# A hybrid decoder trunk: triangular blocks inverted by columns, projection results taken one block later, and a further weight slot

## The chip, the cores and the metric

The kernel runs on one core of one Trainium2 chip. The metric is the device time of one execution, in microseconds (us).

## The reference, cut to what matters

Two post-norm layers over 512 tokens of width 1024. Layer 0 mixes tokens with an RWKV-7 recurrence (8 heads of 64) beside a gated spatial unit; layer 1 with latent attention. Each layer then attends to 256 memory tokens and applies a mixture of 32 experts, of which each token takes two.

```python
def rwkv7_recurrence(r, w, k, v, kk, a):
    def step(state, inp):
        r_t, w_t, k_t, v_t, kk_t, a_t = inp
        sa = jnp.einsum('bhvk,bhk->bhv', state, -kk_t)
        state = (state * w_t[:, :, None, :]
                 + sa[..., None] * (kk_t * a_t)[:, :, None, :]
                 + v_t[..., None] * k_t[:, :, None, :])
        return state, jnp.einsum('bhvk,bhk->bhv', state, r_t)
...
    h = layer_norm(DN_ALPHA * h + mix, ln1_g[layer], ln1_b[layer])
    xa = mem_cross_attention(h, mem, ...)
    h = layer_norm(DN_ALPHA * h + xa, ln2_g[layer], ln2_b[layer])
    ff = hier_moe(h, ...)       # top-1 of 4 groups, top-2 of 8 SwiGLU experts
    h = layer_norm(DN_ALPHA * h + ff, ln3_g[layer], ln3_b[layer])
```

The kernel computes the recurrence in chunks of 128 tokens. For each of 32 pairs (4 chunks, 8 heads) it needs the inverse of a 128 x 128 unit triangular matrix, I minus the strictly triangular part of a product of decayed keys.

## The kernel before

**The mixer's first part** (`mixer`, up to L1019) has two generators that are traced in turns. `prep` (L831 to L943) makes the inverses. It normalises keys (tiles kk, KR, Bn), multiplies them into pab (L872), copies these to Aab, collects the 32 x 32 diagonal blocks in b8 and transposes them (L878, L879), and puts a copy in PSUM (pd). Then it solves all 128 diagonal blocks at once on VectorE, by rows: row i of the inverse (in t8, called tr) is the sum over earlier rows times the entries of row i, one or two products and one reduction for each i (L886 to L893). Four transposes place the blocks in TT, one puts the other orientation in b8 (L900, L902). Larger blocks follow on TensorE: 32 to 64 (pC, pT, L905 to L925), 64 to 128 (pC2, pN2, pT2, L928 to L943), each with copies out of PSUM, most of them on ScalarE. Trace names: pC stands for pC and pC2, pT for pT and pT2, pN for pN2.

`filler` (L1001) is the work that TensorE has meanwhile: projections of x through the columns of `ab_w_in`, in blocks of 128 columns (`proj_cm`, 24 matmuls of 128x512 each, as every fp32 product is made of three). In order: one block for the gate (take_g), four for r (take_r), four for v, then `spatial`: a position-major projection (`proj_tm`, tile ptm, 96 matmuls) whose gelu z is normalised on VectorE, and four blocks with `gate`, which multiply z into pz. Each block's weights are cast on ScalarE (L218) and their low part is made by GpSimd (L219) before the matmuls. `consume` takes the result of a block at once: for r this is a scaling on ScalarE (L760), a shift on VectorE (L761), the product bt (L951) and eight small matmuls into pbn (L956).

**Order.** The framework's planner sets one fixed order for each engine, from the order in which instructions are traced and from when its own durations have their inputs ready. An engine then works its queue strictly in that order. PSUM has two tags of four banks: "a" for `prep`, "b" for `filler`.

**The expert stages** (`moe`) stream 192 weight tiles of 1 MB through a ring of slots, issued by SyncE's queue in the order of use. `wtile` takes the slot at the head of the ring and, unless it is used once only, puts it back at the end. 18 slots are used again and again; two more (the later places of wy and wc) serve one load each. So `ExpertWeights` has n = 20, issues n - 1 loads ahead, and the twentieth when its place is free. Ahead of each stage, `Router` keeps transposed token tiles hT in two half-slots, tags last0 and last1, of which the second first holds the router's weights. At the end of layer 0's stage `early_keys` computes layer 1's memory keys and uses the same two half-slots for kTe.

Of the kernel before, what the change touches and what calls it, by code (L numbers as in the profile page):

```python
# [421 lines left out]

def early_keys(k, l, tag):

    p = k.router.p
    mh, ml = (k.wtile(n, F32R).rearrange("p (k n) -> p k n", k=KD) for n in ("mh", "ml"))
    k.lo_eng, k.nsplit = k.nc.gpsimd, 0
    load_split(k, k.A["memT"], mh, ml, KD, 256)
    yield
    for b, _ in enumerate(memory_keys(k, l, None, lambda h: p.tile([P, D], F32R, name=f"kTe{h}", tag=f"last{h % 2}", bufs=1), mh, ml, tag)):  # L430
        if b == 3:
            k.lo_eng = k.nc.vector
    k.lo_eng, k.nsplit = k.nc.vector, 4
# [126 lines left out]
class Router:  # L560
# [4 lines left out]
    def __init__(self, k, rs, tmp, l, tag):  # L565
        self.k, self.tag, self.tmp = k, tag, tmp
        nc, A = k.nc, k.A
        self.p = p = k.pool(rs, f"hs{l}", side="left")
        self.L = p.tile([P, NT, 36], F32, name="L")

        self.rn = p.tile([P, NT, 3], F32, name="rn")

        self.ch = p.tile([P, 2, KD], F32, name="ch")
        self.hT = {0: self.copy(0)}

        v = self.copy(1).rearrange("p a b -> p (a b)")
# [17 lines left out]
    def copy(self, i):  # L594

        return self.p.tile([P, KD, P], F32, name=f"hT{i}", tag=f"last{i % 2}", bufs=1)

    def weights(self):
        k, nc, V = self.k, self.k.nc, self.k.nc.vector
# [17 lines left out]
    def turn(self, i):  # L617

        k, nc = self.k, self.k.nc
        hT = self.hT[i] = self.hT[i] if i in self.hT else self.copy(i)  # L620
        for q in range(2):
            pt = k.psum(self.tag, name="ptr")
            for j in range(4):
                kk = q * 4 + j
                nc.tensor.transpose(pt[:, j * P:(j + 1) * P], k.h[:, i, kk * P:(kk + 1) * P], k.cst["ident"])
            nc.scalar.copy(hT[:, q * 4:q * 4 + 4, :], pt.rearrange("p (a b) -> p a b", a=4))
# [90 lines left out]
def mixer(k):  # L717
# [6 lines left out]
    with ExitStack() as st:  # L724
# [18 lines left out]
        with ExitStack() as s1:  # L743
# [87 lines left out]
            def prep():  # L831
# [26 lines left out]
                t8 = pool.tile([P, 2048], F32, name="t8")  # L858
                tsum = b8[:, 0:1024].rearrange("p (i u) -> p i u", u=32)
                tr, prod = (t8[:, o:o + 1024].rearrange("p (i u) -> p i u", u=32) for o in (0, 1024))  # L860
                G_.memset(tr, 0.0)
                G_.memset(t8[:, 0:1024:33], 1.0)
                G_.memset(prod, 0.0)
                for x in range(1, 4):
                    G_.memset(TT[32 * x:32 * x + 32, 0:32 * x, :], 0.0)
                for p in range(4):
                    pj = [k.psum("a", name="pab") for j in range(2)]
                    for q in range(NT):
                        qs = slice(q * P, (q + 1) * P)
                        for j in range(2):  # L870
                            r = slice(64 * j, 64 * j + 64)
                            E.matmul(pj[j][:, qs], KR[r, p, 0, qs], Bn[r, p, qs], start=True, stop=True)  # L872
                    for j in range(2):
                        S_.copy(Aab[:, p * 2 + j::8, :], pj[j].rearrange("p (q i) -> p q i", q=NT))
                    yield
                for x in range(4):
                    r = slice(32 * x, 32 * x + 32)
                    (V.tensor_copy if x < 2 else S_.copy)(tsum[r].rearrange("p i u -> p u i"), Aab[r, :, r])  # L878
                V.transpose(b8[:, 1024:], b8[:, 0:1024])  # L879

                dp = [k.psum("a", name=f"pd{n}") for n in range(2)]
                for n in range(2):
                    S_.copy(dp[n], b8[:, 1024 + n * 512:1536 + n * 512])
                dp = [t.rearrange("p (i u) -> p i u", u=32) for t in dp]
                yield
                for i in range(1, 32):  # L886

                    n = min(i, 16)
                    V.tensor_tensor(prod[:, 0:n, 0:n], tr[:, 0:n, 0:n], dp[0][:, 0:n, i, None].to_broadcast([P, n, n]), op=ALU.mult)
                    if i > 16:  # L890
                        V.tensor_tensor(prod[:, 16:i, 0:i], tr[:, 16:i, 0:i],
                                        dp[1][:, 0:i - 16, i, None].to_broadcast([P, i - 16, i]), op=ALU.mult)
                    V.tensor_reduce(tr[:, i, 0:i], prod[:, 0:i, 0:i].rearrange("p j c -> p c j"), axis=AX.X, op=ALU.add)  # L893
                    if i % 2:
                        yield

                S_.copy(prod, tr.rearrange("p i c -> p c i"))
                for x in range(4):
                    r = slice(32 * x, 32 * x + 32)
                    V.transpose(TT[r, r, :].rearrange("p a b -> p (a b)"), t8[r, 0:1024])  # L900
                NT_ = tsum
                V.transpose(b8[:, 0:1024], t8[:, 1024:])  # L902
                yield
                Cs = tr
                for n in range(2):  # L905
                    ps = k.psum("a", name="pC")
                    for u in range(16):
                        for h in (0, 64):
                            r, ri = slice(h + 32, h + 64), slice(h, h + 32)
                            E.matmul(ps[ri, u * 32:u * 32 + 32], Aab[r, n * 16 + u, ri], TT[r, r, n * 16 + u], start=True, stop=True)  # L910
                    for h in (0, 64):
                        ri = slice(h, h + 32)
                        S_.copy(Cs[ri, n * 16:n * 16 + 16, :], ps[ri, :].rearrange("p (u t) -> p u t", t=32))
                    yield
                for n in range(2):
                    ps = k.psum("a", name="pT")
                    for u in range(16):
                        for h in (0, 64):
                            ri = slice(h, h + 32)
                            E.matmul(ps[ri, u * 32:u * 32 + 32], NT_[ri, :, n * 16 + u], Cs[ri, n * 16 + u, :], start=True, stop=True)  # L920
                    for h in (0, 64):
                        ri = slice(h, h + 32)
                        S_.copy(TT[ri, h + 32:h + 64, n * 16:n * 16 + 16].rearrange("p t u -> p u t"),
                                ps[ri, :].rearrange("p (u t) -> p u t", t=32))
                    yield  # L925
                lo, hi = slice(0, 64), slice(64, 128)
                C2, N2 = (x.rearrange("p (u t) -> p u t", t=64) for x in (b8, t8))
                for n in range(4):  # L928
# [8 lines left out]
                    yield  # L937
                for n in range(4):
                    ps = k.psum("a", name="pT2")
                    for u in range(8):  # L940
                        E.matmul(ps[lo, u * 64:u * 64 + 64], N2[lo, n * 8 + u], C2[lo, n * 8 + u], start=True, stop=True)
                    S_.copy(TT[lo, hi, n * 8:n * 8 + 8].rearrange("p t u -> p u t"), ps[lo].rearrange("p (u t) -> p u t", t=64))
                    yield  # L943

            pbn = [None]

# [17 lines left out]
            def spatial():  # L964
# [31 lines left out]
                                    bs[:, None, g * P:(g + 1) * P].to_broadcast([P, NT, P]), op=ALU.add)  # L996
                    G_.tensor_tensor(yb[:, g, :], yb[:, g, :], u, op=ALU.mult)

                yield from proj_cm(k, pool, w_in, 1792, 512, xh, xl, T, "b", gate)

            def filler():  # L1001
                yield from proj_cm(k, pool, w_in, 1664, P, xh, xl, T, "b", take_g)
                yield from proj_cm(k, pool, w_in, 0, 512, xh, xl, T, "b", take_r)
                yield from proj_cm(k, pool, w_in, 1024, 512, xh, xl, T, "b", lambda p, ps: shifted(vv[:, p], ps, 8 + p))
                yield from spatial()

            pr, fl = prep(), filler()
# [1 line left out]
            for n in (2, 2, 2, 2):  # L1009
                next(fl)  # L1010
                for _ in range(n):
                    next(pr)
            for _ in range(5):
                next(fl)
                for _ in range(4):
                    next(pr, None)
            interleave(pr, fl)
            k.lo_eng = V
            k.nsplit = 4  # L1019

# [889 lines left out]
def moe(k, rs, l, last, filler=None):  # L1910
# [3 lines left out]
    with ExitStack() as st:  # L1914
# [6 lines left out]
        n = len(k.rings)  # L1921
        for j in range(EARLY, RD):
            k.ring(rs, f"ring{l}{j}", 1, at=n)
        work = WorkTiles(k, pool)
        st.enter_context(tc.manual_schedule(engines={mybir.EngineType.SP}))
        W = ExpertWeights(k, l)
# [234 lines left out]
```

## Time and profile before

| | |
|---|---|
| Median of 3 runs | 1961.89 us (1961.55 to 1962.85) |
| Profiled execution | 1962.84 us, span from first to last instruction 1961.0 us |
| TensorE busy | 1792.2 us (91% of the span) |
| VectorE, ScalarE, GpSimd busy | 940.4, 535.1 and 278.9 us |
| DMA | 514.69 MB |
| Mean granted TensorE clock | 0.962 |

In the rows below PE is TensorE, PEld its weight loads, DVE VectorE, ACT ScalarE, POOL GpSimd, SPq the DMA issues of SyncE. L872 is line 872 of the kernel. An operand pair such as pab<-Bn,KR names the tile written and those read. Times are from the span's start. [...]

### The profile page before, as it was taken

What the parts mean: (1) busy time and instruction counts of PE and PEld (TensorE: products, weight loads), DVE (VectorE), ACT (ScalarE), POOL (GpSimd) and SP (SyncE); (2) the same over time, 40 slices, a digit from 0 to 9 for tenths busy, and PEclk for the clock granted to TensorE, in tenths of its full rate; (3) what the DMA queues carried; (4) which work ended last, traced back from release to release, by engine and by line L of the source; (5) the groups of instructions that cost most, each with busy time, mean ns of one, the idle gap of its engine ahead of it and who ended that gap; (6) DMA issues with size and microseconds to landing.
All of it is one profiled execution on the core that took longest, in us unless ns stands there. A gap on an engine that the chain in (4) does not pass through costs nothing. (4 is left out here: it accounts for less than half of the span.)

```text
span 1961.0 us, 23938 instructions
## 1 busy us (share of the span) xinstructions
PE 1792.2 (91%) x9222; PEld 1102.1 (56%) x9222; DVE 940.4 (48%) x2142; ACT 535.1 (27%) x996; POOL 278.9 (14%) x279
## 2 busy tenths in 40 slices
PE   8899989999889999989887999989979999999895
PEld 5577867878734443333347766768863434433332
DVE  5686366854723332332335666484472323333326
ACT  6334223343221111111122655343321111111110
POOL 3431532400100000000031100130020000000002
PEclk9897989999989999999999999999989999999997
DMA  5221106364889999999975200343679999999992
GB/s 189 65 65 44 33 23 226 124 217 149 341 330 420 419 421 419 419 420 420 419 283 175 87 20 22 108 141 116 258 294 374 419 420 420 419 420 420 421 418 101
DMA packets 126022, 514.69 MB, mean 262 GB/s; under 512 B 15520, under 2 KB 49472, under 8 KB 77264
## 3 DMA queue, kind: packets, MB, share of 16 engines
q1 hardware_dynamic: 115152, 486.60, 62.9%
q0 software_dynamic: 7056, 18.12, 2.8%
q10 hardware_dynamic: 3696, 8.41, 1.1%
q8 instruction: 74, 1.21, 0.3%
q14 instruction: 44, 0.36, 0.1%
HBM read 506.19 MB, written 14.70 MB: 266 GB/s over the span
## 5 line engine op out<-in xcount | busy, mean ns | idle before, releaser
L1766 PE MATMUL pu<-wu,xT 128*64 128x512 f32 x1024 | 240.9, 594 | 23.7 <-DMA wu<-in_moe_w_up_dram 23.7
L1766 PE MATMUL pg<-wg,xT 128*64 128x512 f32 x1024 | 233.2, 600 | 0.5 <-DMA wg<-in_moe_w_gate_dram 0.5
L1792 PE MATMUL py<-wd,hh 128*64 128x512 f32 x1024 | 228.9, 595 | 0.0
L1799 DVE SCALAR_TENSOR_TENSOR wy<-py,tab,wy 128x512 fp32r<-128x512 f32 x64 | 45.5, 747 | 285.8 <-ACT wy L1798 285.4
L1766 PEld LDWEIGHTS pu<-wu,xT 128*64 128x64 f32 x1024 | 77.4, 137 | 179.6 <-issue 129.7
L1772 DVE TENSOR_TENSOR hh<-hh,pu 128x512 f32<-128x512 f32 x32 | 22.0, 688 | 321.1 <-PE pu L1766 321.1
L1806 PE MATMUL pc<-wy,wc 128*128 128x512 f32 x480 | 139.7, 421 | 27.4 <-DVE h L1816 27.4
L1755 ACT ACTIVATE xT<-px,ch 128x128 f32<-128x128 f32 x128 | 48.2, 457 | 425.4 <-PE px L1748 423.2
L1766 PEld LDWEIGHTS pg<-wg,xT 128*64 128x64 f32 x1024 | 78.0, 139 | 147.9 <-issue 130.8
L1816 DVE TENSOR_TENSOR h<-h,pc 128x512 f32<-128x512 f32 x240 | 151.1, 682 | 8.6 <-PE pc L1806 8.6
L1792 PEld LDWEIGHTS py<-wd,hh 128*64 128x64 f32 x1024 | 71.0, 137 | 133.8 <-issue 128.6
L1806 PEld LDWEIGHTS pc<-wy,wc 128*128 128x128 f32 x480 | 81.6, 189 | 85.9 <-DVE h L1816 50.1
L1730 POOL DMA_INDIRECT xg<-rows,idx x32 | 33.4, 1043 | 532.5 <-PE px L1748 513.1
L1736 ACT ACTIVATE xg<-xg 128x1024 f32<-128x1024 f32 x32 | 39.7, 1240 | 244.8 <-DMA xg<-rows,idx 244.8
L218 ACT CAST wh<-wt 128x1024 fp32r<-128x1024 f32 x50 | 51.8, 1049 | 97.7 <-PE ptm L214 60.7
L219 DVE TENSOR_TENSOR wl<-wt,wh 128x1024 fp32r<-128x1024 f32 x37 | 48.1, 1306 | 58.2 <-ACT wh L218 57.8
L212 PE MATMUL ptm<-wh,oh 128*128 128x512 f32 x192 | 75.6, 394 | 0.0
L213 PE MATMUL ptm<-wl,oh 128*128 128x512 f32 x192 | 75.0, 391 | 0.0
L214 PE MATMUL ptm<-wh,ol 128*128 128x512 f32 x192 | 75.0, 390 | 0.0
L212 PE MATMUL pcm<-xh,wh 128*128 128x512 f32 x144 | 61.4, 426 | 7.7 <-ACT xh L218 7.2
L214 PE MATMUL pcm<-xh,wl 128*128 128x512 f32 x144 | 60.1, 417 | 0.5 <-DVE wl L219 0.5
L213 PE MATMUL pcm<-xl,wh 128*128 128x512 f32 x144 | 60.0, 417 | 0.2 <-DVE xl L219 0.2
(569 smaller groups left out, 3414.7 us busy)
## 6 DMA issues: line engine op xcount, KB each, us to landing
wg<-in_moe_w_gate_dram SPq DMA_DIRECT2D x128, 1024.0 KB, 19.8
wu<-in_moe_w_up_dram SPq DMA_DIRECT2D x128, 1024.0 KB, 20.3
wd<-in_moe_w_down_dram SPq DMA_DIRECT2D x124, 1024.0 KB, 19.9
wr<-in_ab_w_in_dram SPq DMA_DIRECT2D x8, 1024.0 KB, 5.7
wr<-in_xa_wkv_dram SPq DMA_DIRECT2D x8, 1024.0 KB, 11.2
wt<-in_xa_wkv_dram SPq DMA_DIRECT2D x8, 1024.0 KB
wr<-in_xa_wq_dram SPq DMA_DIRECT2D x8, 1024.0 KB, 7.0
wt<-in_xa_wo_dram SPq DMA_DIRECT2D x8, 1024.0 KB
```

The lines of the kernel that those rows point to most:

```text
L212: nc.tensor.matmul(out, lh, rh, start=start, stop=False)
L213: nc.tensor.matmul(out, lh, rl, start=False, stop=False)
L214: nc.tensor.matmul(out, ll, rh, start=False, stop=stop)
L218: k.nc.scalar.copy(hi, src)
L219: (eng or k.low()).tensor_tensor(lo, src, hi.bitcast(F32), op=ALU.subtract)
L1736: self.k.nc.scalar.activation(x[:, :D], x[:, :D], AF.Identity, scale=x[:, D:D + 1], bias=x[:, D + 1:D + 2])
L1755: r = nc.scalar.activation(self.xT[:, kk, :], pk, AF.Identity, scale=gk, bias=bk)
L1766: nc.tensor.matmul(ps[j * M:(j + 1) * M, :], self.xT[:, half * 4 + kk, j * M:(j + 1) * M], w[j][:, kk, :], start=(half == 0 and kk == 0), ...
L1792: nc.tensor.matmul(py[n][j * M:(j + 1) * M, :], self.hT[:, half * 2 + kk, j * M:(j + 1) * M], w[j][:, kk, n * 512:(n + 1) * 512], start=(h ...
L1799: nc.vector.scalar_tensor_tensor(yl, py[n], self.tab()[:, 1:2], yh.bitcast(F32), op0=ALU.mult, op1=ALU.subtract)
L1806: self.k.nc.tensor.matmul(ps, self.C[:, i * P:(i + 1) * P], y, start=start and not last, stop=last)
L1816: k.nc.vector.tensor_add(k.h[:, i, s], k.h[:, i, s], pc)
```

## The change

1. `prep` solves the diagonal blocks by columns. The transposed blocks are masked, kept in prod and copied to PSUM (dp); for m = 1 to 30, column m of prod times row m of dp is written to PSUM (pu) and added to prod's later columns. One copy, one transpose into TD and one into b8 follow; pC reads TD, and GpSimd copies TD's blocks to TT's diagonal.
2. Copies of the larger blocks' results alternate between ScalarE and VectorE. Generators yield at other places, and are interleaved in another order.
3. `late` holds each block's `consume` back until the next block's matmuls are traced.
4. The router's two half-slots become one tile hT, which joins the ring: n = 21, and 19 slots are used again. `early_keys` takes a slot of the ring for its keys.

```diff
 def early_keys(k, l, tag):
-    p = k.router.p
...
-    for b, _ in enumerate(memory_keys(k, l, None, lambda h: p.tile([P, D], F32R, name=f"kTe{h}", tag=f"last{h % 2}", bufs=1), mh, ml, tag)):
+    kT = k.wtile("kTe", F32R)
+    for b, _ in enumerate(memory_keys(k, l, None, lambda h: kT[:, h % 2 * D:(h % 2 + 1) * D], mh, ml, tag)):
@@ Router
-        self.hT = {0: self.copy(0)}
-        v = self.copy(1).rearrange("p a b -> p (a b)")
+        self.place = p.tile([P, 2, KD, P], F32, name="hT", tag="hT", bufs=1)
+        self.hT = {}
+        v = self.place[:, 1].rearrange("p a b -> p (a b)")
...
-        hT = self.hT[i] = self.hT[i] if i in self.hT else self.copy(i)
+        hT = self.hT[i] = self.place[:, i % 2]
@@ mixer, prep
-                G_.memset(tr, 0.0)
-                G_.memset(t8[:, 0:1024:33], 1.0)
-                G_.memset(prod, 0.0)
...
+                dp = [k.psum("a", name=f"pd{n}").rearrange("p (c i) -> p c i", i=32) for n in range(2)]
+                pu = k.psum("a", name="pu")
+                for n in range(2):
+                    V.tensor_tensor(dp[n], c["iota"][:, None, 0:32].to_broadcast([P, 16, 32]),
+                                    c["iota"][:, 16 * n:16 * n + 16, None].to_broadcast([P, 16, 32]), op=ALU.is_gt)
...
-                dp = [k.psum("a", name=f"pd{n}") for n in range(2)]
                 for n in range(2):
-                    S_.copy(dp[n], b8[:, 1024 + n * 512:1536 + n * 512])
+                    hs = slice(16 * n, 16 * n + 16)
+                    V.tensor_tensor(prod[:, hs], b8[:, 1024 + n * 512:1536 + n * 512].rearrange("p (c i) -> p c i", i=32), dp[n], op=ALU.mult)
+                    S_.copy(dp[n], prod[:, hs])
+                V.memset(t8[:, 1024:2048:33], 1.0)
                 yield
-                for i in range(1, 32):
-                    n = min(i, 16)
-                    V.tensor_tensor(prod[:, 0:n, 0:n], tr[:, 0:n, 0:n], dp[0][:, 0:n, i, None].to_broadcast([P, n, n]), op=ALU.mult)
-                    if i > 16:
-                        V.tensor_tensor(prod[:, 16:i, 0:i], tr[:, 16:i, 0:i],
-                                        dp[1][:, 0:i - 16, i, None].to_broadcast([P, i - 16, i]), op=ALU.mult)
-                    V.tensor_reduce(tr[:, i, 0:i], prod[:, 0:i, 0:i].rearrange("p j c -> p c j"), axis=AX.X, op=ALU.add)
-                    if i % 2:
+                for m in range(1, 31):
+                    w = 31 - m
+                    u3 = pu[:, 0:m * w].rearrange("p (c i) -> p c i", i=w)
+                    V.tensor_tensor(u3, dp[m // 16][:, m % 16, None, m + 1:].to_broadcast([P, m, w]),
+                                    prod[:, 0:m, m, None].to_broadcast([P, m, w]), op=ALU.mult)
+                    V.tensor_tensor(prod[:, 0:m, m + 1:], prod[:, 0:m, m + 1:], u3, op=ALU.add)
+                    if m % 5 == 0:
                         yield
-                S_.copy(prod, tr.rearrange("p i c -> p c i"))
-                for x in range(4):
+                V.tensor_copy(tr.rearrange("p i c -> p c i"), prod)
+                NT_, TD = tsum, b8[:, 1024:].rearrange("p (t u) -> p t u", u=32)
+                V.transpose(b8[:, 1024:], t8[:, 0:1024])
+                V.transpose(b8[:, 0:1024], t8[:, 1024:])
+                for x in (1, 3, 0, 2):
                     r = slice(32 * x, 32 * x + 32)
-                    V.transpose(TT[r, r, :].rearrange("p a b -> p (a b)"), t8[r, 0:1024])
-                NT_ = tsum
-                V.transpose(b8[:, 0:1024], t8[:, 1024:])
+                    G_.tensor_copy(TT[r, r, :], TD[r])
                 yield
...
-                            E.matmul(ps[ri, u * 32:u * 32 + 32], Aab[r, n * 16 + u, ri], TT[r, r, n * 16 + u], start=True, stop=True)
-                    for h in (0, 64):
+                            E.matmul(ps[ri, u * 32:u * 32 + 32], Aab[r, n * 16 + u, ri], TD[r, :, n * 16 + u], start=True, stop=True)
+                    for h, cp in ((0, S_.copy), (64, V.tensor_copy)):
...
-                    for h in (0, 64):
+                    for h, cp in ((0, V.tensor_copy), (64, S_.copy)):
...
-                    S_.copy(TT[lo, hi, n * 8:n * 8 + 8].rearrange("p t u -> p u t"), ps[lo].rearrange("p (u t) -> p u t", t=64))
-                    yield
+                    (S_.copy, V.tensor_copy)[n % 2](TT[lo, hi, n * 8:n * 8 + 8].rearrange("p t u -> p u t"),
+                                                    ps[lo].rearrange("p (u t) -> p u t", t=64))
+                    if n % 2:
+                        yield
@@ mixer, filler
-                yield from proj_cm(k, pool, w_in, 1792, 512, xh, xl, T, "b", gate)
+                yield from proj_cm(k, pool, w_in, 1792, 512, xh, xl, T, "b", late(gate))
+                flush()
+            pend = []
+            def flush():
+                while pend:
+                    pend.pop()()
+            def late(consume):
+                def take(*args):
+                    flush()
+                    pend.append(lambda: consume(*args))
+                return take
...
-                yield from proj_cm(k, pool, w_in, 1664, P, xh, xl, T, "b", take_g)
-                yield from proj_cm(k, pool, w_in, 0, 512, xh, xl, T, "b", take_r)
-                yield from proj_cm(k, pool, w_in, 1024, 512, xh, xl, T, "b", lambda p, ps: shifted(vv[:, p], ps, 8 + p))
+                yield from proj_cm(k, pool, w_in, 1664, P, xh, xl, T, "b", late(take_g))
+                yield from proj_cm(k, pool, w_in, 0, 512, xh, xl, T, "b", late(take_r))
+                yield from proj_cm(k, pool, w_in, 1024, 512, xh, xl, T, "b", late(lambda p, ps: shifted(vv[:, p], ps, 8 + p)))
+                flush()
                 yield from spatial()
...
-            for _ in range(5):
+            next(pr)
+            for _ in range(3):
                 next(fl)
-                for _ in range(4):
-                    next(pr, None)
-            interleave(pr, fl)
+                next(pr)
+                next(pr)
+            interleave(fl, pr)
@@ moe
             k.ring(rs, f"ring{l}{j}", 1, at=n)
+        k.rings.append((k.router.p, "hT", 1))
+        rs.callback(k.unring, "hT")
         work = WorkTiles(k, pool)
```

## Rows read from the trace of the kernel before

**Rows 1.** The page, busy tenths in 40 slices of the span.

```profile
PE   8899989999889999989887999989979999999895
```

**Rows 2.** Windows: busy us (instructions) of each engine, granted clock, DMA share, GB/s.

```profile
65.00:75.00 10.00, 5.76 (x30) 2.96 (x28) 9.86 (x9) 2.71 (x4) 6.49 (x4) 0.89 0.30 102
75.00:85.00 10.00, 9.25 (x31) 7.72 (x32) 8.62 (x10) 0.00 (x0) 4.29 (x3) 0.60 0.00 0
...
177.00:196.00 19.00, 19.00 (x124) 16.43 (x124) 15.33 (x54) 6.38 (x8) 2.36 (x1) 0.69 0.17 56
```

**Rows 3.** Waits of TensorE, 0 to 220 us: total us, times, longest.

```profile
PE pbn L956 <- DVE bt L951: 5.1, 4, 2.2
PE pab L872 <- DVE Bn L849: 4.6, 1, 4.6
PE pC L910 <- DVE h L900: 4.1, 1, 4.1
...
PE ptm L212 <- DVE vv L761: 1.4, 1, 1.4
```

**Rows 4.** Timeline of TensorE (start, duration): first and last slow matmul after gaps.

```profile
78.67 0.77 PE L212 MATMUL pcm<-xh,wh 128*128 128x512 f32 x1
...
82.66 0.57 PE L212 MATMUL pcm<-xh,wh 128*128 128x512 f32 x1
...
100.84 0.79 PE L212 MATMUL pcm<-xh,wh 128*128 128x512 f32 x1
...
103.14 0.57 PE L214 MATMUL pcm<-xh,wl 128*128 128x512 f32 x1
...
113.64 0.68 PE L214 MATMUL pcm<-xh,wl 128*128 128x512 f32 x1
...
116.67 0.62 PE L212 MATMUL pcm<-xh,wh 128*128 128x512 f32 x1
...
157.73 0.50 PE L214 MATMUL ptm<-wh,xl 128*128 128x512 f32 x1
...
161.42 0.45 PE L214 MATMUL ptm<-wh,xl 128*128 128x512 f32 x1
```

**Rows 5.** The page's groups: busy us, mean ns, idle before and its releaser.

```profile
L1766 PE MATMUL pu<-wu,xT 128*64 128x512 f32 x1024 | 240.9, 594 | 23.7 <-DMA wu<-in_moe_w_up_dram 23.7
```

**Rows 6.** Groups of VectorE's instructions by line, 105 to 156 us.

```profile
L893 DVE TENSOR_REDUCE t<-t 128x1 f32<-128x1 f32 (+30 forms) x31 | 23.8, 766 | 1.0
L889 DVE TENSOR_TENSOR t<-t,pd 128x256 f32<-128x256 f32 (+15 forms) x31 | 10.3, 332 | 1.5 <-ACT pd L883 0.7
L891 DVE TENSOR_TENSOR t<-t,pd 128x17 f32<-128x17 f32 (+14 forms) x15 | 5.5, 367 | 0.0
```

**Rows 7.** Groups of VectorE by line and shape, 105 to 162 us.

```profile
L889 DVE TENSOR_TENSOR t<-t,pd 128x256 f32<-128x256 f32 x16 | 6.7, 420 | 0.5
L900 DVE STREAM_TRANSPOSE h<-t 32x1024 f32<-32x1024 f32 x4 | 4.9, 1236 | 0.1
...
L891 DVE TENSOR_TENSOR t<-t,pd 128x465 f32<-128x465 f32 x1 | 0.6, 631 | 0.0
```

**Rows 8.** Timeline of VectorE.

```profile
97.51 1.57 DVE L951 SCALAR_TENSOR_TENSOR bt<-r,cv,yb 128x512 f32<-128x512 f32 x1
```

**Rows 9.** Timeline of all engines.

```profile
70.63 2.78 POOL L219 TENSOR_TENSOR wl<-wr,wh 128x1024 fp32r<-128x1024 f32 x1
...
71.14 2.82 DVE L848 SCALAR_TENSOR_TENSOR Bn<-kk,Bn 128x512 f32<-128x512 f32 x1
```

**Rows 10.** Groups of GpSimd's instructions by line, whole span.

```profile
L615 POOL COPY wg<-hT 128x288 f32<-128x288 f32 x2 | 1.2, 600 | 104.4 <-DVE ln_0mv L157 104.4
```

**Rows 11.** DMA rate from 500 to 600 us, in slices of 2.5 us.

```profile
GB/s 419 426 419 418 400 421 413 135 210 0 56 311 385 419 421 420 423 298 217 56 324 128 33 311 419 419 423 419 433 416 403 429 279 367 403 419 426 433 410 426
```

**Rows 12.** Timeline of SyncE's DMA issues.

```profile
556.31 4.24 SPq L104 DMA_DIRECT2D wd<-in_moe_w_down_dram  x4
```

**Rows 13.** Waits of SyncE's queue, from 460 us to the end.

```profile
SPq L104 <- DVE L L651: 11.1, 2, 6.0
```

More of the change, by code (lines that the diff above doesn't have):

```diff
@@ L592, in __init__ @@
             k.ring(rs, f"ring{l}{n}", 1, at=len(k.rings))
-    def copy(self, i):
-        return self.p.tile([P, KD, P], F32, name=f"hT{i}", tag=f"last{i % 2}", bufs=1)
     def weights(self):
@@ L879, in prep @@
                 V.transpose(b8[:, 1024:], b8[:, 0:1024])
-                dp = [k.psum("a", name=f"pd{n}") for n in range(2)]
                 for n in range(2):
-                    S_.copy(dp[n], b8[:, 1024 + n * 512:1536 + n * 512])
-                dp = [t.rearrange("p (i u) -> p i u", u=32) for t in dp]
+                    hs = slice(16 * n, 16 * n + 16)
+                    V.tensor_tensor(prod[:, hs], b8[:, 1024 + n * 512:1536 + n * 512].rearrange("p (c i) -> p c i", i=32), dp[n], op=ALU.mult)
@@ L909, in prep @@
                             r, ri = slice(h + 32, h + 64), slice(h, h + 32)
-                            E.matmul(ps[ri, u * 32:u * 32 + 32], Aab[r, n * 16 + u, ri], TT[r, r, n * 16 + u], start=True, stop=True)
-                    for h in (0, 64):
+                            E.matmul(ps[ri, u * 32:u * 32 + 32], Aab[r, n * 16 + u, ri], TD[r, :, n * 16 + u], start=True, stop=True)
+                    for h, cp in ((0, S_.copy), (64, V.tensor_copy)):
                         ri = slice(h, h + 32)
-                        S_.copy(Cs[ri, n * 16:n * 16 + 16, :], ps[ri, :].rearrange("p (u t) -> p u t", t=32))
-                    yield
+                        cp(Cs[ri, n * 16:n * 16 + 16, :], ps[ri, :].rearrange("p (u t) -> p u t", t=32))
+                yield
                 for n in range(2):
@@ L920, in prep @@
                             E.matmul(ps[ri, u * 32:u * 32 + 32], NT_[ri, :, n * 16 + u], Cs[ri, n * 16 + u, :], start=True, stop=True)
-                    for h in (0, 64):
+                    for h, cp in ((0, V.tensor_copy), (64, S_.copy)):
                         ri = slice(h, h + 32)
-                        S_.copy(TT[ri, h + 32:h + 64, n * 16:n * 16 + 16].rearrange("p t u -> p u t"),
-                                ps[ri, :].rearrange("p (u t) -> p u t", t=32))
-                    yield
+                        cp(TT[ri, h + 32:h + 64, n * 16:n * 16 + 16].rearrange("p t u -> p u t"),
+                           ps[ri, :].rearrange("p (u t) -> p u t", t=32))
+                yield
                 lo, hi = slice(0, 64), slice(64, 128)
@@ L936, in prep @@
                     V.tensor_copy(N2[lo, us], ps[1][lo].rearrange("p (u t) -> p u t", t=64))
-                    yield
+                    if n % 2:
+                        yield
                 for n in range(4):
@@ L941, in prep @@
                         E.matmul(ps[lo, u * 64:u * 64 + 64], N2[lo, n * 8 + u], C2[lo, n * 8 + u], start=True, stop=True)
-                    S_.copy(TT[lo, hi, n * 8:n * 8 + 8].rearrange("p t u -> p u t"), ps[lo].rearrange("p (u t) -> p u t", t=64))
-                    yield
+                    (S_.copy, V.tensor_copy)[n % 2](TT[lo, hi, n * 8:n * 8 + 8].rearrange("p t u -> p u t"),
+                                                    ps[lo].rearrange("p (u t) -> p u t", t=64))
+                    if n % 2:
+                        yield
             pbn = [None]
```

## The prediction

> **What bounds the kernel now.** The page's 40 slices come first [rows 1]: TensorE is at 8 tenths or more in all but three of them, so the end moves when TensorE idles less, runs at a higher clock, or waits less for weights. The change touches two places: the mixer's substitution stretch, some 55 to 215 us, and the number of weight slots of the expert stages.
>
> Mixer: the windows of 10 us [rows 2] show TensorE with 5.76 us of work from 65 to 75, then a granted clock of 0.60 for 10 us, and 0.69 from 177 to 196, where the small matrices of the block inverse run between projection blocks. The waits of TensorE up to 220 us [rows 3] name what is late: the row sums of the bonus (pbn) wait 5.1 us in four pieces for VectorE's product bt; pab waits 4.6 us once for Bn; the first pC waits 4.1 us for VectorE's transposes at the end of the substitution; the position-major projection waits 1.4 us for vv. That is 15.2 us. [...] Slow ones start 0.43 us apart (eight of them from 113.64 to 116.67), fast ones 0.23. I count 10 slow starts behind the gap at 71 us, 6 behind that at 97, 8 behind that at 111 and 9 behind that at 153: 33 x 0.20 = 6.6 us.
>
> So VectorE's long substitution costs the end only its tail: TensorE has the projections' blocks to do meanwhile (24 matmuls at 0.23 us, 5.5 us each). It stands before pC only because its fixed order puts four pC ahead of ten projection matmuls that then run from 157.73 us on [rows 4].
>
> Expert stages: TensorE waits 23.7 us for wu over the two [rows 5], with DMA at about 420 GB/s [rows 11]. So they end with the last weight, and what counts is how many megabytes are in SBUF before the first slot is given back.
>
> **The change part by part.** *Substitution by columns.* Before, between 105 and 156 us, 31 reductions take 23.8 us and 46 products 10.3 + 5.5 us [rows 6], 39.6 in all. After, each of 30 steps is a product and a sum over m(31-m) elements, 4,960 over all steps, at most 240 in one. A product of 256 takes 0.42 us, one of 465 takes 0.63 [rows 7]: 0.16 + 0.00101 n. With 0.04 us more between dependent instructions (estimated), 60 x 0.20 + 2 x 4,960 x 0.00101 = 22.0 us. A product written to PSUM by VectorE is in no row; nearest are the products that read pd there. Bounds: 60 x 0.10 us more, or nothing. I take nothing. The two masks, the two multiplications by them (0.68 each by the same line) and the copies to pd add 2.0 us. Behind it one copy of 1.1 us and one transpose stand before pC, in place of two of four transposes that take 4.9 together [rows 7]. The chain shortens by 17.6 - 2.0 us, some 15; by bounds 9 to 16.
>
> [...]
>
> *What of it reaches TensorE.* At most the 4.1 us before pC. Each engine's order is fixed by a planner's own durations, and they put pC some 4 us early here. With a chain of 35 us in place of 50, the error shrinks, and four filler blocks are left behind it in the new interleaving. I take 3 us; bounds -3 (it waits longer) and 4.1.
>
> *Results one block later.* take_r's pbn now stands behind the next block's 24 matmuls, 5.5 us, while its product takes 1.57 us [rows 8] behind two steps of some 0.7. So bt is there: 4.5 of the 5.1 us go. If the cover were gone the 5.1 would stay. vv is drained when VectorE is freer: 0.7 of 1.4. The pab wait comes from VectorE's queue: it holds a product of 2.82 us, from 71.14 on, that ends when GpSimd's wl ends [rows 9], then r's shift, then the last product of Bn. Delaying r takes some 0.7 us out; if block r1 is also planned before pab, all 4.6 are covered, if not, 4 remain. Half: 2.3, bounds 0 and 4.6.
>
> *Clock.* With the pbn gaps gone, 14 of the 33 slow starts go (2.8 us); of the 19 after the other two gaps half (1.9). I take 4.7, bounds 0 and 6.6. The small matrices still run at the low clock; cut into pieces between filler blocks they may leave more slow starts behind them, six pieces x 8 x 0.20 = 9.6 us against 4.6 (23 slow starts after 157, 175 and 189 us), so I subtract 2.
>
> *Copies on two engines.* ScalarE's copies of pC, pT and pT2 are hidden but for two waits under 0.5 us: I take 0.5. VectorE gains six copies of 0.6 to 1.1 us. TT's diagonal goes to GpSimd: four copies of 1,024 elements. Its copy of 288 takes 0.60 us [rows 10], so about 2.1 each, 8.5 together; bounds 0.6 and 2.78 (its wl of 1,024 with two inputs [rows 9]). Ahead of pC2, which needs them, stand pC, pT and two filler blocks, 18 us: hidden. Behind a wl of 2.8 us still some 7 us would be spare.
>
> *One more slot.* hT's two halves become a 1 MB slot, so 21 loads can be issued in place of 20 before a slot is reused, and 19 in place of 18 afterwards. Reuse starts at 556.31 us [rows 12], and DMA stands nearly idle before it (217, 56, 324, 128, 33 GB/s in slices of 2.5 us from 545) [rows 11]. There is room for one load more. hT is free once the last logits are read, and the queue waits for those in any case just before (L651 [rows 13]). Afterwards one megabyte less is to move at 420 GB/s: 2.5 us per stage, 5.0 for both, bounds 0 and 5.0. The first stage's kT takes one of the 21, at the tail, when loads are done: nothing.
>
> *Sum*, against the profiled execution's 1962.8 us (span 1961.0 and 1.8 around it): 3 + 4.5 + 0.7 + 2.3 + 4.7 - 2 + 0.5 + 5.0 = 18.7. I subtract 0.7 for added mask and order work, so 18: 1944.8 us. The median of the runs is 0.95 lower: 1943.9, forecast 1944.
>
> **The rivals.** *All of it comes*: every wait of [rows 3] goes, with its slow starts, and the slots: 15.2 + 6.6 + 0.5 + 5 = 27, so 1934.6. For it speaks that all four waits of [rows 3] are for VectorE, which the change unloads. Against it: the pab wait is not of the substitution's making. [...]
>
> *Only the slots and pbn*: the planner again misplaces pC and pab, and the clock falls as before: 5 + 4.5 less new waits of 4, so 1956. For it: in the trace TensorE stands because of fixed orders, not for want of work.
>
> *No change*: the mixer's gain is lost to new waits of some 15 us, or the substitution's wait moves to the four hand-overs; 1959 to 1965.
>
> *Slower*: VectorE works its queue in order and now holds half of the copies from pC to pT2, while it also has the normalisation of z, 15.33 us of work between 177 and 196 [rows 2]. If a copy stands behind a piece of it that waits for z, TensorE stands at that hand-over. With 5 us of waiting and 2 of low clock at each of four, 28 us, the result is 1962 - 18 + 28 = 1972; it decides from about 22 us on. Against it: the orders are planned with z's readiness in view.
>
> A further help to that rival is the collision of [rows 9]: 2.82 us for a VectorE product of 512 while GpSimd works, and GpSimd gets four copies more. Eight products and sums of z could wait for them, 8.5 us at most, under four filler blocks of 22. [...]
>
> **How the numbers follow.** Chances: forecast (1938 to 1950) 0.45; all of it 0.17; only slots and pbn 0.24; no change 0.06; slower 0.08. A measurement of this kernel tells 0.2%, 3.9 us, from no change. The first three are faster by more than that: 0.86; same 0.06; slower 0.08. The range leaves out what lies well beyond "all of it" and the last two: 1928 to 1957.
>
> **What would show it.** The profile after should have no wait of pbn for bt, 30 pairs of VectorE instructions of at most 0.42 us in some 22 to 28 us, four GpSimd copies near 2 us, the mixer's last pz some 13 us earlier than 217 us, and the first reuse of a weight slot with one load more before it; each expert stage from its first pg to its last py 2.5 us shorter. The prediction is wrong if TensorE's idle time in the stretch stays near 15 us, if new waits for VectorE's copies stand before pT or pC2, or if the slot's load waits for hT and delays those behind it in the queue.

## The result and the profile after

| | before | after |
|---|---|---|
| Median | 1962.37 us (1961.55 to 1964.22, 4 runs) | 1943.49 us (1940.64 to 1946.41, 4 runs) |
| Ratio after / before | | 0.9905, 95% interval 0.9891 to 0.9919 |
| Profiled execution: span | 1961.0 us | 1944.6 us |
| TensorE waits for wu, both stages | 23.7 us | 19.3 us |

The kernel is 18.6 us faster (0.0095 x 1962.4); 1944 was forecast. The profiled execution of after is the slowest of its four (1946.41), so the traces differ by 16.4 us. The first and last instructions of named tiles on TensorE cut this difference into stretches (prn is the first tile of `prep`, pz the last of the mixer's first part; pg opens an expert stage and py closes it):

| stretch on TensorE | before | after | difference |
|---|---|---|---|
| start to the first prn | 61.33 | 62.86 | +1.5 |
| first prn to the last pz (the change in the mixer) | 156.92 | 146.42 | -10.5 |
| to the last logits of the first routing | 314.62 | 317.19 | +2.6 |
| to the first pg (routing) | 18.39 | 19.89 | +1.5 |
| first pg to last py (expert stage 1) | 461.49 | 459.79 | -1.7 |
| to the last logits of the second layer | 436.76 | 428.64 | -8.1 |
| to the first pg (routing) | 18.80 | 19.99 | +1.2 |
| expert stage 2 | 462.29 | 459.41 | -2.9 |

The change was expected to act in the mixer and in the two stages; 8.1 us come from a place for which nothing was forecast, and routing became longer.

**The mixer.** The waits of TensorE from 50 to 215 us, against [rows 3]:

```profile
PE pbn L961 <- DVE bt L956: 5.7, 2, 5.3
PE pz L999 <- DVE z L992: 4.9, 2, 3.5
...
PE pab L867 <- DVE kk L841: 1.7, 1, 1.7
```

The waits of pC and of vv are gone. That of pbn is not: it was 5.1 us in four pieces and is now one of 5.3 and a small one. pz has a new wait for the normalised z. Timelines of VectorE and of GpSimd before it:

```profile
181.91 3.08 DVE L990 TENSOR_SCALAR z<-z,zmv,zry 128x128 f32<-128x128 f32 x3
...
186.37 0.85 DVE L990 TENSOR_SCALAR z<-z,zmv,zry 128x128 f32<-128x128 f32 x3
```

```profile
182.47 2.44 POOL L219 TENSOR_TENSOR wl<-wr,wh 128x1024 fp32r<-128x1024 f32 x1 [6.52 <-ACT wh L218]
```

Beside a wl, three pieces of z take 3.08 us in place of 0.85. The same windows as in [rows 2]:

```profile
65.00:75.00 10.00, 10.00 (x35) 5.90 (x34) 8.34 (x7) 1.66 (x3) 6.34 (x4) 1.00 0.34 107
75.00:85.00 10.00, 3.65 (x29) 2.68 (x27) 10.00 (x12) 2.60 (x4) 4.94 (x5) 0.85 0.00 0
85.00:95.00 10.00, 9.38 (x40) 7.93 (x41) 3.29 (x3) 1.07 (x2) 4.46 (x3) 0.64 0.34 105
...
177.00:196.00 19.00, 14.13 (x59) 11.47 (x58) 17.21 (x34) 4.13 (x5) 7.07 (x3) 0.87 0.24 83
```

The idle time moved from the first window into the second, where VectorE is busy for 10.00 of 10 us, and the low clock follows it into the third: 0.64, where 1.00 is full speed. VectorE's queue there, timeline:

```profile
72.67 2.88 DVE L846 SCALAR_TENSOR_TENSOR Bn<-kk,Bn 128x512 f32<-128x512 f32 x1
75.48 0.73 DVE L841 SCALAR_TENSOR_TENSOR kk<-Kh,cv,pkk 128x512 f32<-128x512 f32 x1
...
82.57 0.74 DVE L759 SCALAR_TENSOR_TENSOR r<-pcm,cv,r 128x511 f32<-128x511 f32 x1
83.23 0.68 DVE L847 TENSOR_TENSOR Bn<-Bn,vv 128x512 f32<-128x512 f32 x1
83.83 1.74 DVE L956 SCALAR_TENSOR_TENSOR bt<-r,cv,yb 128x512 f32<-128x512 f32 x1
```

All products of kk, KR and Bn for the four blocks, but for Bn's last, stand ahead of r's shift. The matmuls of r's first block end at 69.27 us, but the shift begins at 82.57 and bt ends at 85.57: one block of 5.7 us cannot hide that.

The substitution, VectorE's groups by line from 105 to 136 us, against [rows 6]; then GpSimd's copies of TT, timeline:

```profile
L892 DVE TENSOR_TENSOR pu<-pd,t 128x30 f32<-128x30 f32 (+14 forms) x30 | 10.1, 338 | 0.9
L894 DVE TENSOR_TENSOR t<-t,pu 128x30 f32<-128x30 f32 (+14 forms) x30 | 9.8, 326 | 0.9
```

```profile
138.12 4.28 POOL L904 COPY h<-b 32x1024 f32<-32x1024 f32 x4
```

19.9 us of work and 1.8 of gaps, where before it was 39.6 of work; 1.07 us a copy of TT. From the last pab to the first pC it takes 39.2 us in place of 56.5.

The clock. Windows of the mixer's whole stretch and of its part from the first pC to the first pz, in which the small matrices of the inverse run; before, then after:

```profile
61.33:218.25 156.92, 141.32 (x934) 115.23 (x935) 97.77 (x190) 52.68 (x65) 52.95 (x26) 0.86 0.16 51
157.41:196.50 39.09, 38.77 (x443) 33.80 (x444) 22.59 (x75) 16.78 (x22) 4.73 (x2) 0.65 0.09 29
```

```profile
62.86:209.28 146.42, 134.20 (x934) 109.76 (x935) 90.29 (x182) 45.80 (x58) 58.15 (x30) 0.91 0.17 55
138.16:186.77 48.61, 48.61 (x521) 41.30 (x520) 22.99 (x70) 15.81 (x20) 13.61 (x8) 0.89 0.17 56
```

TensorE's waits fell only from 15.2 to 12.3 us. Most of the 10.5 us, 7.1, is in the work itself: the same 934 matmuls take 134.2 us in place of 141.3, at a mean granted clock of 0.91 in place of 0.86, and the clock rose most where the small matrices run. Run 3 shows it again (135.8 us, 0.90); run 5, the columns alone, does not (141.2 us, 0.85). Of the rest of the mixer's change (order, copies on two engines, later results) no run shows which part raised the clock.

**The second layer.** In the trace of before, VectorE's timeline and the waits of TensorE from 1050 to 1075 us; then VectorE's timeline in that of after:

```profile
1056.41 2.69 DVE L219 TENSOR_TENSOR wl<-win,wh 128x544 fp32r<-128x544 f32 x4 [0.18 <-ACT wh L218]
1065.65 3.21 DVE L219 TENSOR_TENSOR hl<-pth,hh 128x512 fp32r<-128x512 f32 x5 [6.55 <-DMA keys<-kTe]
```

```profile
PE pth L254 <- DVE hl L219: 7.4, 1, 7.4
```

```profile
1048.98 2.48 DVE L219 TENSOR_TENSOR hl<-pth,hh 128x512 fp32r<-128x512 f32 x4 [1.14 <-ACT hh L218]
```

Before, hl waits 6.55 us for the transfer that stores kT, and TensorE's transposes 7.4 us for hl. After, with kT in the ring, hl waits 1.14 us, for ScalarE.

**Expert stages.** The page's group that answers to [rows 5]:

```profile
L1787 PE MATMUL pu<-wu,xT 128*64 128x512 f32 x1024 | 237.8, 594 | 19.3 <-DMA wu<-in_moe_w_up_dram 19.3
```

### The profile page after: what moved, and what is told of

It reads as the page before. It is cut to its first block, busy times and chain, and to the rows that moved or that the text cites. A ratio compares the mean times of both kernels' runs of the same rounds, so it can differ in the third digit from the quotient of the medians.

```text
span 1944.6 us, 23927 instructions
## 1 busy us (share of the span) xinstructions
PE 1785.4 (92%) x9222; PEld 1095.1 (56%) x9222; DVE 932.9 (48%) x2134; ACT 527.8 (27%) x989; POOL 283.8 (15%) x280
## 5 line engine op out<-in xcount | busy, mean ns | idle before, releaser
L1787 PE MATMUL pu<-wu,xT 128*64 128x512 f32 x1024 | 237.8, 594 | 19.3 <-DMA wu<-in_moe_w_up_dram 19.3
L218 ACT CAST wh<-wt 128x1024 fp32r<-128x1024 f32 x50 | 51.8, 1050 | 92.2 <-PE ptm L214 56.6
```

The costliest lines, as they stand in the source:

```text
L218: k.nc.scalar.copy(hi, src)
L1787: nc.tensor.matmul(ps[j * M:(j + 1) * M, :], self.xT[:, half * 4 + kk, j * M:(j + 1) * M], w[j][:, kk, :], start=(half == 0 and kk == 0), ...
```

## The experiments

Times are medians of 4 to 6 runs; "gain" is one minus the ratio to the kernel before, times 1963 us, with its 95% interval.

**1. kT alone.** Before with the change of `early_keys` only:

```diff
-lambda h: p.tile([P, D], F32R, name=f"kTe{h}", tag=f"last{h % 2}", bufs=1)
+lambda h: kT[:, h % 2 * D:(h % 2 + 1) * D]   with kT = k.wtile("kTe", F32R)
```

> The kernel before, with only the early keys' tile kT taken from the ring of weight slots in place of hT's memory; mixer and number of slots as before. Theory: before, the first hl of the second layer's attention is written where kT lay, so VectorE waits 6.6 us for the last store of keys, and TensorE's transposes pth wait 7.4 us for hl. Without it 6 to 8 us go: about 1955, and the profile's wait of pth for hl is under 2 us. Rival: the start of that attention then waits for its own weights (win), or the slot that kT takes delays a load there; under 2 us go: 1960 to 1962.

Measured 1954.42 us, gain 7.3 (4.7 to 10.0). The wait of pth for hl is 0.9 us, and the stretch from py of stage 1 to the logits shrinks by 9.6 us. The theory holds: this term, which the prediction put at nothing, is over a third of the whole gain.

**2. kT and the slot.** As 1, with the tile hT and its place in the ring.

> The kernel before with kT from the ring and with the 21st slot, the mixer as before. Theory: the slot takes 2 to 2.5 us out of each expert stage, 4 to 5 in all, on top of the run with kT alone: about 1950, TensorE's wait for wu falls from 23.7 to 19 us. Rival: the first load into hT's memory waits for the logits and delays the queue behind it, so the stretch of routing grows by 1.2 to 1.5 us per layer and the slot is worth 2 us or less: 1953 to 1955.

Measured 1952.08 us, gain 10.0 (7.5 to 12.8): 2.3 to 2.7 more than 1, between the two ranges and closer to the rival's. Its stages are 2.2 and 2.7 us shorter than in 1, as forecast, but the routings are 2.0 and 1.6 longer. The rival's reason does not show: SyncE's queue waits 5.5 us for the first layer's logits both with the slot and without it, and 5.7 and 5.6 in the second. What routing waits for is the gather of the first tokens: GpSimd issues it, ScalarE scales its rows. Timelines of kT alone:

```profile
544.21 1.54 POOL L1730 DMA_INDIRECT xg<-rows,idx  x1 [9.70 <-DMA wu<-in_moe_w_up_dram]
...
549.39 1.24 ACT L1736 ACTIVATE xg<-xg 128x1024 f32<-128x1024 f32 x1 [9.85 <-DMA xg<-rows,idx]
```

and with the slot:

```profile
543.20 1.54 POOL L1728 DMA_INDIRECT xg<-rows,idx  x1 [9.70 <-DVE xTs L1693]
...
550.33 1.24 ACT L1734 ACTIVATE xg<-xg 128x1024 f32<-128x1024 f32 x1 [11.81 <-DMA xg<-rows,idx]
```

From issue to scaling it takes 5.2 us with 20 slots and 7.1 with 21. In the traces of the four kernels with 20 slots (before, 1, 3, 5) the eight values lie between 5.0 and 5.3; in those with 21 whose loads were issued in the order of the change, between 6.2 and 8.1 us. In the 18 us ahead of the gather SyncE issues six loads in the former and seven in the latter; that the seventh holds up the gather is what runs 11 and 12 test.

**3. The mixer alone.** After without the slot, kT in hT's memory.

> The changed kernel without its slot and with kT in hT's memory: the whole change of the mixer alone. Theory: the mixer's stretch is 10.5 us shorter and nothing later gives it back: about 1951.5. Rival: later stretches take up part of it (loads that were hidden behind the mixer): 1955 or more.

Measured 1954.45 us, gain 8.2 (5.5 to 11.2). Its waits are those of after (pbn 5.7, pz 4.8). In its trace the mixer is 8.9 us shorter than before and the stretch to the first logits 3.8 longer, so the rival, that later stretches take part of it up, is nearer than the theory. In the trace of after that stretch grew by 2.6 us: 1.0 of them is the first layer's pth waiting longer for hl (4.2 us in place of 3.2), the rest stands in no wait. The three parts (7.3, 2.7, 8.2) add up to 18.2 of the 18.6 us.

**4. Results two blocks later.** After, with

```diff
 def flush():
     while pend:
-        pend.pop()()
+        pend.pop(0)()
 def take(*args):
-    flush()
+    if len(pend) > 1:
+        pend.pop(0)()
     pend.append(lambda: consume(*args))
```

> The changed kernel with the projections' results taken two blocks later in place of one. Theory: the row sums of the bonus then stand behind another block and no longer wait 5.7 us for VectorE's queue of products, and the gate's first product pz no longer waits 4.9 us for the normalised z; with the low clock behind both gaps 10 to 13 us go against the changed kernel: 1930 to 1934. Rival: VectorE's queue is the bound in both places, so the wait of pbn comes back as a wait of pab for Bn, and that of pz at the next gate block; 0 to 4 us go: 1939 to 1944.

Measured 1928.23 us, gain 34.7 (32.2 to 37.3): 15 us better than after, beyond the theory's 10 to 13. From 62 us to the last pz its trace has no wait of TensorE above 0.2 us; its windows:

```profile
75.00:85.00 10.00, 10.00 (x92) 8.90 (x94) 9.96 (x11) 5.51 (x9) 6.90 (x4) 1.00 0.00 1
85.00:95.00 10.00, 10.00 (x54) 8.35 (x53) 9.74 (x9) 5.99 (x7) 5.13 (x3) 1.00 0.34 106
```

VectorE is as full as before, but TensorE has another block to do, and the clock stays at 1.00. The last pab ends at 85.4 us in place of 99.0, the last pz at 193.1 in place of 209.3.

**5. Columns alone.** Before with the new substitution and GpSimd's copies, everything else as before.

> The kernel before with the substitution by columns alone (one transpose in place of four, GpSimd's copies of TT); order of the work, copies of the larger blocks, time of the results, kT and slots as before. Theory of the prediction: VectorE's chain is some 15 us shorter, but only the wait of pC for it, 4.1 us, meets TensorE, and 3 us of it go: 1958 to 1961. Rival: a shorter chain lets the whole stretch close up and brings what the mixer alone brought: 1953 to 1956. Rival: pC is only put earlier and waits again: 1962 to 1964.

Measured 1955.77 us, gain 7.1 (4.3 to 9.6). The waits of pC and vv, 5.5 us, are gone; from 62 us on

```profile
PE pbn L960 <- DVE bt L955: 5.1, 4, 3.2
PE pab L869 <- DVE Bn L849: 4.6, 1, 4.6
```

stay as in [rows 3]. The first rival's range was met: the columns bring most of what the mixer brings. In the trace the mixer's stretch is 5.7 us shorter, which is these two waits.

**6. After with results at once.** `late` returns `consume` itself.

> The changed kernel with the projections' results taken at once. Theory: one block later bought nothing, since the wait of pbn for bt stayed (5.1 us before, 5.7 after): 1941 to 1946 against 1943.5 of the changed kernel. Rival, the prediction's: it hid most of pbn's wait and the gate's, so without it 5 to 8 us come back: 1948 to 1952.

Measured 1946.37 us, gain 17.5 (14.5 to 20.4), against 18.6 of after. Waits of TensorE:

```profile
PE pab L867 <- DVE Bn L847: 4.6, 1, 4.6
PE pbn L961 <- DVE bt L956: 4.4, 3, 3.2
PE pz L999 <- DVE z L992: 3.1, 2, 2.5
```

12.1 us of waits here, 12.3 in after: one block later moves them and does not remove them, as the theory said. The prediction's 5 to 8 us are not seen; the medians differ by 2.9 us, 0.4 more than the theory's range allows, and the runs of both overlap. What one block later does to the clock this pair leaves open: the trace here has 140.2 us of matmuls in the mixer, at a clock of 0.85, but it is of an execution 6.7 us above the median of its four.

**7. r alone two blocks later.** As 4 for `take_r`; g, v and the gate one block later.

> The changed kernel with r's results alone taken two blocks later (g's, v's and the gate's one block later as in the change). Theory: pbn's wait for bt (5.7 us) and its low clock go, 8 to 10 us, while pz's wait for z (4.9 us) stays: 1933 to 1936. Rival: with TensorE earlier by 8 us the wait for z grows by as much, since z depends on VectorE's queue: 1938 to 1943.

Measured 1941.03 us, gain 21.8 (18.3 to 25.3). pbn's wait falls to 1.3 us and pz's stays at 4.8. The last pz is 5.7 us earlier than in after, the median only 2.5, within the scatter (1938.1 to 1946.9). The theory's 8 to 10 us fell. The time is in the rival's range, but the rival's reason does not show: the wait for z did not grow. Of 13.7 us that the last pab gained, 8 were gone by pz. Between pab and pC 4.1 more than in 4 go to that wait and a stretch at a low clock from 99.3 us (0.72 on average from 95 to 105 us, in 4 1.00), and from pT2 to pz it takes 32.6 us, in 4 25.6. So r alone is not enough: g, v and the gate, which 4 delays as well, bring 13 us more together, and the wait for z is the gate's.

**8. Rows with results two blocks later.** Before with kT, the slot and the edit of 4, the substitution as before.

> The kernel before with the slot, kT from the ring and results two blocks later, but substitution by rows, four transposes and the larger blocks' copies as before. Theory: once the waits for bt are gone TensorE comes to pC some 15 us before the chain by rows ends, so the columns are needed for the gain of two blocks later; new waits of pC of 5 us or more: 1938 to 1946. Rival: the filler covers the chain by rows as well, and only its tail of 4 us shows: 1930 to 1935.

Measured 1940.63 us, gain 23.6 (20.6 to 26.5). The waits of TensorE:

```profile
PE pC L908 <- DVE h L898: 4.1, 1, 4.1
PE ptm L212 <- DVE vv L759: 2.9, 1, 2.9
```

The time is in the theory's range, but pC waits 4.1 us as before, not 5 or more: the filler covers the rest of the chain by rows, as the rival said. These two waits make up 7.0 of the 8.0 us by which the mixer is longer than in 4. The kernels differ in more than the columns: here the larger blocks' copies and the interleaving are as before too. So in 4 these parts together are worth 11 us (34.7 - 23.6), against 7 of the columns by themselves in 5; they unload VectorE's queue, in which vv stands as well as pC's input.

**9. The product in SBUF.** As 4, but

```diff
-u3 = pu[:, 0:m * w].rearrange("p (c i) -> p c i", i=w)
+u3 = b8[:, 0:m * w].rearrange("p (c i) -> p c i", i=w)
```

> The kernel with results two blocks later, with the 30 products of the substitution written to SBUF in place of PSUM, so that the 30 sums read both inputs from SBUF. [...] Theory from the rows: the durations stay (0.18 to 0.40), a few sums stretch to over 1 us, and since TensorE no longer waits in this stretch the time stays: 1926 to 1931. Rival: the chain becomes longer than TensorE's cover and pC waits 3 us or more: 1932 to 1936.

Measured 1941.00 us: 12.8 slower than 4. The theory, that the time stays, fell, and the rival's range is exceeded. Timelines of VectorE and of GpSimd:

```profile
97.23 1.86 DVE L894 TENSOR_TENSOR t<-t,b 128x84 f32<-128x84 f32 x1
...
102.21 2.17 DVE L894 TENSOR_TENSOR t<-t,b 128x130 f32<-128x130 f32 x1
...
105.48 2.42 DVE L894 TENSOR_TENSOR t<-t,b 128x168 f32<-128x168 f32 x1
```

```profile
96.60 2.38 POOL L219 TENSOR_TENSOR wl<-wr,wh 128x1024 fp32r<-128x1024 f32 x1 [6.47 <-ACT wh L218]
...
101.38 2.85 POOL L219 TENSOR_TENSOR wl<-wr,wh 128x1024 fp32r<-128x1024 f32 x1
105.31 2.40 POOL L219 TENSOR_TENSOR wl<-wr,wh 128x1024 fp32r<-128x1024 f32 x1 [1.09 <-ACT wh L218]
```

Each of the three sums ends 0.1 to 0.2 us after the wl beside it; two more (2.22 and 2.03 us) end 0.3 after theirs. In 4, with the product in PSUM, the same sum takes its usual time at the same moment:

```profile
97.23 0.24 DVE L894 TENSOR_TENSOR t<-t,pu 128x84 f32<-128x84 f32 x1
```

Five sums lose some 9 us, and the shift of vv, behind them in the queue, keeps TensorE waiting 7.7 us. The last pz comes 8.1 us later than in 4. The other 4.7 between the medians cannot be read from these traces: that of 4 is of an execution 5.5 us above its median, and the two traced executions differ by only 7.5.

**10. A load behind the gather, by the order alone.** As 4, the 20th load traced under `issue_after` of the first scaling.

> The kernel with results two blocks later, with the last load of the first fill of the weight slots issued only when the first gather of tokens has been scaled. Theory: the 21st slot gives part of its gain back because the stream of loads is a megabyte longer and the gather lands 2 us later behind it; moved behind the gather, each routing stretch is 1 to 1.5 us shorter and the megabyte still comes in before the first reuse: 1925 to 1927 against 1928.2. Rival: the transfer engines then stand idle for the length of one load, so the slot's 2.5 us per stage is lost: 1930 to 1933.

Measured 1927.19 us, gain 35.9 (32.8 to 39.1). The trace shows the loads issued as in 4 (the 20th, which should have moved, 5.9 us ahead of the gather; scaling after 7.7 and 7.0 us), so the edit took no effect, and the run says nothing on either theory. It is 4 once more, and shows the scatter: its trace has 128.8 us for the mixer's stretch, that of 4 132.7.

**11. A load behind the gather, by data.** As 4, with two loads fewer at first and, behind the first scaling, a load that `wchunk` lets wait for the gathered rows xg0:

```diff
-W.load()
+W.load(X[0].xg0[:, 0:1])
+W.load()
+W.load()
...
 t = self.wtile(name)
+if after is not None:
+    self.nc.scalar.copy(t[:, 0:1], after)
```

> The kernel with results two blocks later, with the 19th load of each expert stage made to wait for the first gather: ScalarE, once it has scaled the gathered rows, writes one column of them into the slot that this load then overwrites; the two loads behind it follow. Theory: with 20 slots the gather's rows are scaled 5.0 to 5.3 us after its issue, with 21 after 6.2 to 8.1; with this load out of the way it is 5.3 or less again, each routing stretch is 1 to 2 us shorter, and the megabyte is in before the first reuse of a slot: 1924 to 1926 against 1928.2. Rival: the megabyte comes too late and the slot's gain in the stage (2 to 2.7 us each) is lost: 1929 to 1932. Second rival: the gather is slow for another reason, it stays above 6 us, and nothing is gained.

Measured 1921.67 us, gain 38.3 (33.6 to 43.0). The first gathers are scaled after 4.8 and 5.2 us, the routings are 1.5 and 2.1 us shorter than in 4, the stages 0.6 and 0.9 longer: 2.1 us net by the traces, and neither rival shows. The median lies below the theory's range. The rest of the 6.6 between the medians is not explained by this edit: the mixer takes 128.3 us, as in 10, and the granted clock of its profiled execution in the windows of 10 us from 125 to 165 us is 0.81, 0.68, 1.00 and 1.00, in that of 4 0.76, 0.67, 0.84 and 0.71. It is the fastest kernel of the study, but its interval overlaps that of 4.

**12. The same on the mixer of before.** As 2, with the edit of 11.

> The kernel before with kT from the ring and the 21st slot, its mixer as before, and with the 19th load of each expert stage waiting for the first gather as in the run on the kernel with results two blocks later. Theory: the slot is worth its 2.5 us per stage, and what it lost was the gather's: with 2 to 4 us of gather back over both layers the kernel comes to 1948 to 1950, against 1952.1 with the slot alone and 1954.4 with kT alone; the gather's rows are scaled 5.3 us or less after its issue. Rival: the gain of the earlier run was that of the clock in its mixer and of its other stretches, not of the gather: 1951 to 1954.

Measured 1950.41 us, gain 12.4 (9.8 to 14.9), 1.7 better than 2 by the medians. Scaling of its first gather:

```profile
548.89 1.24 ACT L1736 ACTIVATE xg<-xg 128x1024 f32<-128x1024 f32 x1 [9.62 <-DMA xg<-rows,idx]
```

after an issue at 543.95: 4.9 us, and 5.3 in the second layer. Against 2, whose mixer is the same, the routings are 2.0 and 1.6 us shorter and the stages 0.8 and 0.9 longer. With it the slot brings 4.0 to 5.1 us over 1, near the 5.0 forecast. The median lies between the two ranges, and the intervals of 2 and 12 overlap, so the medians support the theory without settling its size; the gather's times are plain.

## Why the prediction was right

The time was right by luck, since wrong terms cancelled: the mixer brought 8.2 us (5.5 to 11.2) where 13 were summed, kT 7.3 where nothing was, and the slot 2.7 where 5.0 were. Two of the prediction's own signs speak against its mechanism: pbn still waits for bt, and TensorE's waits in the mixer stay at 12.3 us, near the 15 that it named as a sign of being wrong. The last pz comes 9.0 us earlier, not 13.

- **Substitution.** 22.0 us were estimated, 19.9 of work and 1.8 of gaps measured (0.03 for each of the 60 instructions, where the estimate had 0.04). A step of 240 elements takes 0.42 and 0.40 us, as the line through [rows 7] said, so taking no price for the product in PSUM was right. The chain became 17 us shorter, not 15. Its worth at TensorE, 3 us for pC and 0.7 for vv, was too small: both waits go whole (5.5), and alone the columns bring 7.1.
- **pbn, -4.5.** This step failed. "So bt is there" compared bt's own 1.57 us with a block of 5.5. It left out what VectorE's fixed order puts ahead of r's shift: the products of kk, KR and Bn of all blocks, to 82.6 us. Runs 4 and 6 show both sides: at once and one block later the waits of pab, pbn and pz add up to 12.1 and 12.3 us; two blocks later they are gone.
- **pab, -2.3.** The wait fell by 2.9, since r1 was indeed put ahead of pab; but the idle time reappeared at pbn.
- **z.** The mechanism of the slower rival came in part: VectorE, stretched by GpSimd's wl (3.08 us in place of 0.85), is late with z, and pz waits 4.9 us. The price was far from the 28 us of that rival.
- **Clock, -4.7 and +2.** The slow matmuls that were counted start 0.43 us apart, fast ones 0.23, and stand at a granted clock of 0.51 (78.67 to 83.10 us), 0.50 (100.84 to 103.40), 0.52 (113.64 to 116.67) and 0.57 (157.73 to 161.70) in the trace of before. As the early gaps stayed, so did the low clock behind them: 0.64 from 85 to 95 us, where before it was 0.60 from 75 to 85, and 0.86 on average from the first prn to the last pab in both traces. But with the small matrices between blocks the clock rose, where 2 us were charged for its fall: 0.89 in place of 0.65. By the two traces the clock is worth 7.1 us where 2.7 were summed, and the waits 2.9 where 10.5 were (3, 0.7, 4.5 and 2.3); these sizes are of single executions, and runs 4 and 10 differ by 4 us with one mixer. So inside the mixer, too, a wait that stayed was made up by a clock that rose.
- **TT's copies** took 1.07 us each, where 2.1 were estimated, and were hidden as said.
- **Slot, -5.0.** The stages lost 1.7 and 2.9 us, about the 2.5 each. What was missing is the price: the load comes in together with the first gather, and routing grew by 1.5 and 1.2. Runs 11 and 12 keep the load behind the gather: it takes 4.8 to 5.3 us again, and each routing is 1.5 to 2.1 us shorter.
- **kT, "nothing".** The loads were indeed done. The step that failed looked at the slot that kT takes and not at the memory that it leaves: there hl was written next, and had to wait for the last store of keys. Run 1 shows it.

Run 9 has both inputs of a sum in SBUF: its sum of 128x84 takes 0.25 us where no wl runs and 1.86 beside one, and ends 0.1 us after it. A price of a PSUM source does not show: undisturbed sums take 0.19 to 0.41 us with both inputs in SBUF (run 9) and 0.18 to 0.40 with one in PSUM (run 4).

## What to carry to other kernels

A result that was taken one block later, 5.7 us, was not covered here: the products ahead of its producer kept VectorE until 82.57 us, and pbn waited 5.3 us. So add up what stands ahead of the producer on its engine, as well as the producer's own time, and try a delay of two where one only moves the wait (run 4: no wait above 0.2 us). A tile that moves to other memory frees its old place: look who writes there next, and which transfer that writer waits for (hl in the trace of before: 6.55 us). Another buffer brings its transfer forward into something, here into a short gather that the next stage waits for (7.1 us from issue to scaling in run 2, 5.2 in run 1).

## What was not expected of the hardware

The first gather of a stage, 128 rows, takes 5.0 to 5.3 us from issue to use with six weight loads issued in the 18 us ahead of it, 6.2 to 8.1 with seven, and 4.8 to 5.3 with five; each load alone is 1 MB, at the 420 GB/s of [rows 11] by estimate 2.5 us. And a temporary in PSUM protected this VectorE chain: the same sum took 0.24 us beside GpSimd's wl with one input in PSUM (after, at 109.07 us, beside a wl of 2.40 from 108.44 on), and 1.86 us with both in SBUF (run 9).
